# Ten projection chunks of up to 512 columns become eight: regrouping the input projection of a two-layer decoder trunk

## The chip, the cores and the metric

The kernel runs on one core of one Trainium2 chip. The metric is the device time of one execution in microseconds (us); lower is better. A core has five engines with a queue each: TensorE (PE, with its weight loads listed as PEld), VectorE (DVE), ScalarE (ACT), GpSimd (POOL) and SyncE (SP), which here issues most of the DMA transfers. Each engine works through its own queue in order and waits for others at semaphores.

## What is computed

Two layers of a decoder trunk on 256 tokens of 1024 channels, in float32. In each layer one input projection feeds three attentions and all gates:

```python
h = rms_norm(x, norm_g)
proj = h @ w_in                                  # 256 x 1024 times 1024 x 7058
(mq, mk, mv, mz, nq, kc, vc, ksl, vsl, kw, vw, ng, nz,
 fq, fk, fv, ff, fz, gl) = jnp.split(proj, offsets, axis=-1)
...
y_moba = (o_moba * jax.nn.silu(mz)) @ w_up_moba      # o_moba: 6 heads of mq, mk, mv
...
y_nsa = (o_nsa * jax.nn.silu(nz)) @ w_up_nsa         # o_nsa: 4 heads of nq, three gated branches
...
log_f = jax.nn.log_sigmoid((ff + b_f).astype(jnp.float32)).transpose(0, 2, 1)
o_fox = merge_heads(fox_attention(q, k, split_heads(fv, FOX_HEADS), log_f))
y_fox = (o_fox * jax.nn.silu(fz)) @ w_up_fox
g = jax.nn.sigmoid(gl + b_gate).reshape(B, S, N_BRANCH, D_MODEL)
merged = g[:, :, 0] * y_moba + g[:, :, 1] * y_nsa + g[:, :, 2] * y_fox
return x + merged @ w_out
```

The fox attention adds to its scores the running sum of log_f at the query less that at the key, so every query needs the running sums of all keys, per head.

## The kernel before

**Dense products.** The 256 tokens are two halves (t = 0, 1) of 128. Both factors of a product are split into a high part of type float32r and the rest, and `mm3` (lines 286 to 289) adds three matmuls: high by high, high by low, low by high. A chunk of w_in of n columns takes 8 row blocks x 2 halves x 3 = 48 matmuls of n columns (`dense`, line 294). Its accumulators are two PSUM banks (`new_acc`, 291) of a pool of four, so a chunk takes over the banks of an earlier chunk once those are evacuated.

**Weights.** A chunk is loaded in tiles of two row blocks (`chunk` 229, `load` 246; staging pool `wst` of six). ACT rounds a tile to its high part (line 262), DVE subtracts it (line 263); `prefetch` has four such tiles split ahead of use.

**Order on PE.** PE's order is written out by hand; Tile orders the other engines' instructions. `run` (1072) lists the chunks. After each step of 3 matmuls, `tick` advances a planner's clock by 3 x n x 0.00042 us, and every unit of work (a generator) that has come due adds its next piece; the yields (LAG_Q = 10, LAG_F = 9 and so on) are the planner's us between a unit's steps. `finish` advances the clock by 0.25 us at a time, with no dense work, until the units named are done.

The chunks are a (queries and compressed tokens of nsa, 512 columns), mv 384, b (396), mq 384, mz 384, mk 384, fv 384, fq 384, fz (ff and fz, 390), fk 384, with the four parts w0 to w3 of the compression weights in between, then six chunks gl0 to gl5 of 512 for the gates gl, then the up projections and the output projection.

**What follows a chunk.** `evac` (439) scales columns of an accumulator by the row's norm into SBUF on ACT. `qk_post` (525) norms and rotates six heads of queries or keys and, LAG_Q later, transposes them. `v_post` and `z_post` evacuate values and output gates. `cmp_post` (773) runs behind w3; the first heads (`nsa_heads`) start when it is done, then the compressed heads (`cmp_heads`, whose PV product is line 857 and waits for a copy `pc`, line 850), then the moba heads and the fox heads. At most two pairs of heads run at a time, and their PV products (lines 587 to 591) keep their order.

**Forget gates.** `fz_post` (863) computes log_f by a series of small DVE operations (lines 870 to 888), sums it along the tokens by three matmuls (891 to 893), writes the sums to DRAM (899) and reads them back to all 128 partitions as `ck` by two broadcasts on ACT's queue (900, 901). DVE adds the causal mask to two of ck's three blocks of 128 columns (908, 909). `attend` (550) takes ck as a bias for the fox heads (line 562).

**Pages.** Pool `pgs` has 12 pages of 4 KB a partition. om (2), hT (4), z (2), mv, fv, Z (2, until w3 is done) and the gates gl (2 per branch, taken by the evacuations in line 926 of gl0, gl2 and gl4) share it.

Of the kernel before, what the change touches and what calls it, by code (L numbers as in the profile page):

```python
# [29 lines left out]
C_NQ, C_KW = 1536, 2048  # L30
C_FQ, C_FK, C_FV, C_FF = 2444, 2828, 3212, 3596
C_GL = 3986
# [61 lines left out]
def trunk(ctx, tc, x, w_in, b_gate, cmp_w1, w_up_moba, w_up_nsa, w_up_fox, w_out, gains_d, eye_d, x_t, small_d, row_d, out):  # L94
# [134 lines left out]
    def chunk(blocks, n):  # L229

        out_ = []
        for block in blocks:
            kk = max(b for _, b, _ in block)
            m = 1024 // n
            for k in range(0, kk, m):
                w_ = {"n": n, "m": min(m, kk - k), "at": len(tiles), "loads": []}
                for a, b, src in block:
                    a1, b1 = max(a, k), min(b, k + m)
                    if a1 < b1:
                        for r, s_ in src if isinstance(src, tuple) else ((slice(0, 128), src),):  # L240
                            w_["loads"].append((r, a1 - k, b1 - k, s_[:, a1 - a:b1 - a]))
# [108 lines left out]
    def layer(l):  # L350
# [139 lines left out]
        def k_cols(k, hi, lo, t, pairs, key):  # L490

            p3, g = cols_of(k, pairs, key)
            for (r, o, d), (_, _, e) in zip(halves(hi, t), halves(lo, t)):
                A.activation(d[r], p3[r], AF.Copy, scale=g[r])
                V.scalar_tensor_tensor(e[r], p3[r], g[r], d[r].bitcast(F32), op0=ALU.mult, op1=ALU.subtract)
                A.activation(d[o], p3[r], AF.Copy, scale=g[r])  # L496

        def shared_cols(k, b, t, key):
# [26 lines left out]
        def qk_post(key):  # L525
# [5 lines left out]
            for t in range(NT):  # L531
                sumsq(ss, ps, t, 0, 6)
            qs = heads_scaled(ps, head_factors(ss, 6), 0, 6, key)
            yield LAG_Q
            for t in range(NT):
                if key[1] == "k":
                    k_cols(qs[t], *sh["T_" + key], t, 3, key)
                else:
                    q_cols(qs[t], *sh["T_" + key], t, 3, key)
                yield LAG_T  # L540

        def v_post(key):
            ps = sh["ps_" + key]
            sh[key] = pgs.tile([128, NT, 384], F32, name="v", tag="page")
            for t in range(NT):
                evac(ps, t, 0, 384, sh[key][:, t, :])
            yield 0
# [159 lines left out]
        def post_b():  # L707
# [45 lines left out]
        def load_w1(i):  # L753
            src = tuple((slice(kv * 64, kv * 64 + 64),
                         cmp_w1[l, kv, i * 8 * HD:(i + 1) * 8 * HD, :].rearrange("(i d) n -> d i n", d=HD))
# [107 lines left out]
        def fz_post():  # L863
            ps = sh["ps_fz"]
            xf = sm.tile([128, NT, FH], F32, name="xf")
# [4 lines left out]
            for t in range(NT):  # L870
                V.scalar_tensor_tensor(xf[:, t, :], ps[t][:, 0:FH], sh["r"][:, t:t + 1], bfb[:, l, :],
                                       op0=ALU.mult, op1=ALU.add)
# [3 lines left out]
            for t in range(NT):  # L876
                evac(ps, t, FH, 384, sh["z"][t][:, 640:1024])

# [113 lines left out]
        def mm_out(parts, between):  # L992
# [18 lines left out]
            for t in range(NT):  # L1011
                for n in range(2):
# [9 lines left out]
        parts = {}  # L1022
        PROJ = {"a": (C_NQ, 512), "b": (C_KW, 396), "mq": (C_MQ, 384), "mk": (C_MK, 384), "mv": (C_MV, 384),
                "mz": (C_MZ, 384), "fq": (C_FQ, 384), "fk": (C_FK, 384), "fv": (C_FV, 384), "fz": (C_FF, 390)}
        ORDER = ["a0", "a1", "mv0", "mv1", "b0", "w0", "b1", "mq0", "w1", "mq1", "w2", "mz0", "mz1", "w3",
                 "mk0", "mk1", "fv0", "fv1", "fq0", "fq1", "fz0", "fz1", "fk0", "fk1"]

        def queue_loads():
            for o in ORDER:
                name, b = o[:-1], int(o[-1])  # L1030
                if name == "w":
                    parts[o] = load_w1(b)
                else:
                    c0, n = PROJ[name]
                    m = 1 if l == 0 and name == "a" else 4
                    parts[o] = chunk([[(i, i + m, rows_of(w, 4 * b + i, 4 * b + i + m, c0, n))
                                       for i in range(0, 4, m)]], n)
            sh["gls"] = [load_gl(c) for c in range(6)]
            sh["ups"] = [load_up(n) for n in range(2)]
            sh["outs"] = load_out()  # L1040

        def mm(o, starts=None):
            name = o[:-1]
            if name == "w":
                return mm_w1(int(o[-1]), parts[o])
            n, h = PROJ[name][1], int(o[-1])
            if h == 0:
# [18 lines left out]

        def z_post():
            for t in range(NT):
                evac(sh["ps_mz"], t, 0, 384, sh["z"][t][:, 0:384])
            yield 0  # L1070

        def run(starts, following):
# [9 lines left out]
            mm("mv1")  # L1082
            uv = unit(v_post("mv"))
            if l == 0:
# [93 lines left out]
```

## Time and profile before

| | us |
|---|---|
| median of three runs | 518.43 |
| lowest, highest | 517.68, 518.47 |
| the profiled execution, whole | 517.28 |
| its span, from the first to the last instruction | 515.5 |
| PE busy in the span | 501.9 (97%) |
| DVE busy | 401.5 (78%) |
| ACT busy | 334.6 (65%) |

The profile records one execution. Busy is the time in which an engine has an instruction under way; matmuls are pipelined, so their printed lengths overlap, and the distance between starts tells what one of them costs the queue. "Idle before" is the time an engine stood before an instruction, and the arrow behind it names what released it. The chain of waits follows the last instruction back through whatever released each step.

### The profile page before, as it was taken

The numbers are of one execution on the slowest core, as the hardware profiler recorded it, in microseconds if no ns is written. First come the engines' busy times: TensorE is split into PE (matmuls) and PEld (weight loads), VectorE is DVE, ScalarE is ACT, GpSimd is POOL, SyncE is SP. The second block draws the span as 40 slices with busy tenths as digits, with TensorE's granted clock in tenths as the row PEclk, the third lists the DMA queues.
The fourth block names the chain that finished last, engine by engine and source line by source line (L and its number), as shares of the span: only waits on it lengthen the run. The fifth ranks groups of instructions, "written<-read, shape, count | busy, mean of one in ns | idle before, by whom it ended". The sixth has DMA issues, their size and how long they took to land.

```text
span 515.5 us, 8244 instructions
## 1 busy us (share of the span) xinstructions
PE 501.9 (97%) x2822; PEld 446.6 (87%) x2822; DVE 401.5 (78%) x846; ACT 334.6 (65%) x645; POOL 60.5 (12%) x84
## 2 busy tenths in 40 slices
PE   8899999999999999999999999999998999999997
PEld 6788999999788888888889989999987888888886
DVE  4799988789876658998497998768997755698953
ACT  4887676976675576654276976678757666655440
POOL 3510211000110005025100000000011000042300
PEclk9999999999999999999999999999999999999999
DMA  8999886555585443756557898647556643537502
GB/s 279 332 243 256 237 246 194 148 166 162 164 257 144 124 129 116 219 163 190 144 145 207 202 244 268 173 127 202 154 182 189 194 130 116 164 117 226 180 9 81
DMA packets 60226, 93.09 MB, mean 181 GB/s; under 512 B 3980, under 2 KB 34840, under 8 KB 60184
## 3 DMA queue, kind: packets, MB, share of 16 engines
q1 hardware_dynamic: 56592, 89.67, 59.7%
q10 hardware_dynamic: 3592, 2.90, 1.7%
q8 instruction: 22, 0.36, 0.3%
q14 instruction: 20, 0.16, 0.1%
HBM read 91.49 MB, written 1.06 MB: 180 GB/s over the span
## 4 chain that ended last, share of the span: by engine, by line
PE 81%; DVE 8%; ACT 5%; DMA 3%; issue 3%; ACTq 0%; DVEq 0%; SPq 0%
PE acc L287 22%; PE acc L289 21%; PE acc L288 21%; DVE wl L263 4%; PE at L579 2%; DMA st<-in_w_in_dram 2%; ACT wh L262 2%; PE at L565 2%; PE at L566 2%; PE at L336 1%; PE o L587 1%; PE o L589 1%; PE o L591 1%; PE at L473 1%; PE o L768 1%
## 5 line engine op out<-in xcount | busy, mean ns | idle before, releaser
L263 DVE TENSOR_TENSOR wl<-st,wh 128x1024 fp32r<-128x1024 f32 (+4 forms) x180 | 200.3, 1120 | 53.7 <-ACT wh L262 52.0
L262 ACT ACTIVATE wh<-st 128x1024 fp32r<-128x1024 f32 (+4 forms) x180 | 170.2, 953 | 86.9 <-PE acc L289 68.0
L287 PE MATMUL acc<-wh,hT 128*128 128x512 f32 (+4 forms) x560 | 216.8, 387 | 1.4 <-ACT wh L262 1.0
L288 PE MATMUL acc<-wl,hT 128*128 128x512 f32 (+4 forms) x560 | 202.6, 362 | 0.9 <-DVE wl L263 0.9
L289 PE MATMUL acc<-wh,lT 128*128 128x512 f32 (+4 forms) x560 | 203.0, 362 | 0.0
L289 PEld LDWEIGHTS acc<-wh,lT 128*128 128x128 f32 x560 | 105.1, 188 | 10.9
L287 PEld LDWEIGHTS acc<-wh,hT 128*128 128x128 f32 x560 | 105.8, 189 | 9.2 <-ACT wh L262 1.4
L288 PEld LDWEIGHTS acc<-wl,hT 128*128 128x128 f32 x560 | 105.9, 189 | 7.8 <-DVE wl L263 1.5
L574 ACT ACTIVATE p<-p,nm 128x128 f32<-128x128 f32 x80 | 35.6, 446 | 24.4 <-DVE nm L572 24.3
L940 POOL TENSOR_TENSOR z<-z,tmp 128x512 f32<-128x512 f32 x8 | 12.9, 1645 | 109.0 <-ACT tmp L937 109.0
L287 PE MATMUL acc<-wh,qkT 128*128 128x512 f32 x64 | 25.6, 400 | 0.0
L289 PE MATMUL acc<-wh,qkT 128*128 128x512 f32 x64 | 25.0, 391 | 0.0
L288 PE MATMUL acc<-wl,qkT 128*128 128x512 f32 x64 | 25.0, 390 | 0.0
L978 POOL TENSOR_TENSOR mg<-mg,tmp 128x512 f32<-128x512 f32 x8 | 15.8, 1997 | 51.5 <-DVE tmp L977 51.5
L579 PE MATMUL at<-ident,p 128*128 128x128 f32 x120 | 19.8, 274 | 0.3
L926 DVE SCALAR_TENSOR_TENSOR gl<-acc,rt,tmp 128x512 f32<-128x512 f32 x24 | 17.3, 745 | 1.8 <-PE o L591 1.1
L579 PEld LDWEIGHTS at<-ident,p 128*128 128x128 f32 x120 | 15.0, 146 | 2.5 <-ACT qkT L496 0.6
L572 DVE CUSTOM_DVE_ANT_0 p<-at,tabs 128x128 f32<-128x128 f32 (+1 forms) x56 | 17.0, 354 | 0.1
L583 DVE COPY pt<-at 128x384 f32<-128x384 f32 x20 | 11.1, 555 | 7.2 <-PE at L579 7.0
L768 PE MATMUL o<-wh,Z 128*63 128x256 f32 x64 | 15.6, 282 | 0.4 <-DVE Z L744 0.3
L581 ACT ACTIVATE pt<-at 128x384 f32<-128x384 f32 x20 | 9.7, 483 | 9.5 <-PE at L579 9.4
L769 PE MATMUL o<-wl,Z 128*63 128x256 f32 x64 | 15.4, 280 | 0.2 <-DVE wl L263 0.2
(238 smaller groups left out, 690.9 us busy)
## 6 DMA issues: line engine op xcount, KB each, us to landing
st<-in_w_in_dram SPq DMA_DIRECT2D x52, 512.0 KB, 3.6
st<-in_w_in_dram SPq DMA_DIRECT2D x56, 384.0 KB, 4.1
st<-in_cmp_w_dram SPq DMA_DIRECT2D x32, 256.0 KB, 4.7
st<-in_w_out_dram SPq DMA_DIRECT2D x16, 512.0 KB, 3.8
st<-in_w_in_dram SPq DMA_DIRECT2D x8, 396.0 KB, 6.9
st<-in_w_in_dram SPq DMA_DIRECT2D x8, 390.0 KB, 3.2
tmp<-in_b_gate_dram SPq DMA_DIRECT2D x12, 256.0 KB, 4.4
st<-in_w_up_moba_dram SPq DMA_DIRECT2D x4, 512.0 KB, 3.6
```

The source lines that it names most:

```text
L262: return (lambda: A.activation(h, s_, AF.Copy), lambda: V.tensor_tensor(lo, s_, h.bitcast(F32), op=ALU.subtract))
L263: lambda: V.tensor_tensor(lo, s_, h.bitcast(F32), op=ALU.subtract))
L287: T.matmul(ps, sh, wh, start=first, stop=False)
L288: T.matmul(ps, sh, wl, start=False, stop=False)
L289: T.matmul(ps, sl, wh, start=False, stop=last)
L572: V.tensor_tensor_reduce(out=u, in0=sp, in1=add[t], scale=-SCALE, scalar=BIG, op0=ALU.add, op1=ALU.min, accum_out=nm)
L574: exps.append(A.activation(u, u, AF.Exp, bias=nm, scale=-1.0, accum_out=rsum[:, t, hb:hb + 1]))
L579: T.transpose(pts[:, s * 128:(s + 1) * 128], p[:, s * 128:(s + 1) * 128], ident)
L768: T.matmul(U, st, h, start=i == 0, stop=False)
L769: T.matmul(U, st, lo, start=False, stop=i == CL - 1)
L926: V.scalar_tensor_tensor(sh["gl"][t][b][:, n * 512:(n + 1) * 512], ps[t], sh["r"][:, t:t + 1], bg, op0=ALU.mult, op1=ALU.add)
L978: (G if b == 1 else V).tensor_tensor(m, m, tmp, op=ALU.add)
```

## The change

The ten projection chunks ahead of gl become eight. Six of them are filled to 512 columns: mv, b and mq each take a piece of mz; mk and fq a piece of fv; fk a piece of fz. The fifth chunk, ff (402 columns), holds the first 128 columns of fv, ff, 256 columns of fz and the last 12 of mz; it stands where mz stood, and `fz_post` follows it. gl0 moves ahead of fk. A tile's columns can now come from several ranges of w_in, by one DMA each. Evacuations follow the pieces. ck is filled by one broadcast; the mask sums read the block that it fills, in `mask_sums`, which is ordered behind the first half of fk's key columns.

```diff
-C_FQ, C_FK, C_FV, C_FF = 2444, 2828, 3212, 3596
+C_FQ, C_FK, C_FV, C_FF, C_FZ = 2444, 2828, 3212, 3596, 3602
...
-        for i, (r, a, b, src) in enumerate(w_["loads"]):
-            queues[i % len(queues)].dma_start(v[r, a:b], src)
+        for i, (r, a, b, c, src) in enumerate(w_["loads"]):
+            queues[i % len(queues)].dma_start(v[r, a:b, c], src)
...
             for t in range(NT):
                 sumsq(ss, ps, t, 0, 6)
+            for t in range(NT):
+                if key == "mq":
+                    evac(ps, t, 384, 128, sh["z"][t][:, 244:372])
+                elif key == "fk":
+                    evac(ps, t, 384, 128, sh["z"][t][:, 896:1024])
+                else:
+                    c = 128 if key == "mk" else 256
+                    evac(ps, t, 384, 128, sh["fv"][:, t, c:c + 128])
             qs = heads_scaled(ps, head_factors(ss, 6), 0, 6, key)
             yield LAG_Q
             for t in range(NT):
                 if key[1] == "k":
-                    k_cols(qs[t], *sh["T_" + key], t, 3, key)
+                    i = k_cols(qs[t], *sh["T_" + key], t, 3, key)
+                    if key == "fk" and t == 0:
+                        mask_sums(i)
...
-        def v_post(key):
+        def v_post():
...
+                evac(ps, t, 384, 128, sh["z"][t][:, 0:128])
...
                 evac(ps, t, 140, 256, sh["z"][t][:, 384:640])
+                evac(ps, t, 396, 116, sh["z"][t][:, 128:244])
...
         def fz_post():
-            ps = sh["ps_fz"]
+            ps = sh["ps_ff"]
+            sh["fv"] = pgs.tile([128, NT, 384], F32, name="v", tag="page")
...
-                evac(ps, t, FH, 384, sh["z"][t][:, 640:1024])
+                evac(ps, t, 0, 128, sh["fv"][:, t, 0:128])
+                evac(ps, t, 128 + FH, 256, sh["z"][t][:, 640:896])
+                evac(ps, t, 390, 12, sh["z"][t][:, 372:384])
...
-            nc.scalar.dma_start(sh["ck"][:, :, 0:128], csd[:, 0:128][None].to_broadcast([128, FH, 128]))
             nc.scalar.dma_start(sh["ck"][:, :, 128:384], csd[None].to_broadcast([128, FH, S]))
...
+        def mask_sums(last):
+
             mask = tabs[:, K_MASK + 128:K_MASK + 256][:, None, :].to_broadcast([128, FH, 128])
-            for i in (0, 256):
-                V.tensor_tensor(sh["ck"][:, :, i:i + 128], sh["ck"][:, :, i:i + 128], mask, op=ALU.add)
+            for i, j in ((0, 128), (256, 256)):
+                after(V.tensor_tensor(sh["ck"][:, :, i:i + 128], sh["ck"][:, :, j:j + 128], mask, op=ALU.add), [last])
...
-        ORDER = ["a0", "a1", "mv0", "mv1", "b0", "w0", "b1", "mq0", "w1", "mq1", "w2", "mz0", "mz1", "w3",
-                 "mk0", "mk1", "fv0", "fv1", "fq0", "fq1", "fz0", "fz1", "fk0", "fk1"]
+        PROJ = {"a": [(C_NQ, 512)], "mv": [(C_MV, 384), (C_MZ, 128)], "b": [(C_KW, 396), (C_MZ + 128, 116)],
+                "mq": [(C_MQ, 384), (C_MZ + 244, 128)], "ff": [(C_FV, 128), (C_FF, 262), (C_MZ + 372, 12)],
+                "mk": [(C_MK, 384), (C_FV + 128, 128)], "fq": [(C_FQ, 384), (C_FV + 256, 128)],
+                "fk": [(C_FK, 384), (C_FZ + 256, 128)]}
+        ORDER = ["a0", "a1", "mv0", "mv1", "b0", "w0", "b1", "mq0", "w1", "mq1", "w2", "ff0", "ff1", "w3",
+                 "mk0", "mk1", "fq0", "fq1", "gl0", "fk0", "fk1"]
...
+        def columns(ranges, k0, k1):
+            at = 0
+            out_ = []
+            for c0, n in ranges:
+                out_.append((slice(0, 128), slice(at, at + n), rows_of(w, k0, k1, c0, n)))
+                at += n
+            return tuple(out_)
...
             mm("w2")
-            mm("mz0")
-            mm("mz1")
-            unit(z_post())
+            mm("ff0")
+            mm("ff1")
+            uf = unit(fz_post())
             mm("w3")
...
-            mm("fv0")
-            mm("fv1")
-            uv = unit(v_post("fv"))
             mm("fq0")
             mm("fq1")
             uq = unit(qk_post("fq"))
-            mm("fz0")
-            mm("fz1")
-            uf = unit(fz_post())
+            mm_gl(0, sh["gls"][0])
             mm("fk0")
             mm("fk1")
             uk = unit(qk_post("fk"))
             hf = pairs(heads3("fq", "fk", "fv", 0, 640, True) + heads3("fq", "fk", "fv", 1, 640, True),
-                       [uq, uk, uv, uf])
+                       [uq, uk, uf])
             every = hs + h2 + [hc] + hm + hf
-            for c in range(5):
+            for c in range(1, 5):
                 mm_gl(c, sh["gls"][c])
             finish(*every)
```

## Rows read from the trace of the kernel before

**Rows 1.** The page: busy shares, granted clock in 40 slices, the chain by engine.

```profile
PE 501.9 (97%) x2822; PEld 446.6 (87%) x2822; DVE 401.5 (78%) x846; ACT 334.6 (65%) x645; POOL 60.5 (12%) x84
...
PEclk9999999999999999999999999999999999999999
...
PE 81%; DVE 8%; ACT 5%; DMA 3%; issue 3%; ACTq 0%; DVEq 0%; SPq 0%
```

**Rows 2.** Timeline of PE, chunk of 384 columns (start, length, engine, line, form).

```profile
84.58 0.34 PE L287 MATMUL acc<-wh,hT 128*128 128x384 f32 x1
...
86.66 0.33 PE L287 MATMUL acc<-wh,hT 128*128 128x384 f32 x1
```

**Rows 3.** Timeline of PE, chunk gl5 of 512 columns.

```profile
203.66 0.39 PE L289 MATMUL acc<-wh,lT 128*128 128x512 f32 x1
...
206.61 0.39 PE L287 MATMUL acc<-wh,hT 128*128 128x512 f32 x1
```

**Rows 4.** Timeline of PE: layer 0's last PV, and the first matmul of gl5.

```profile
195.46 0.33 PE L591 MATMUL o<-v,pt 128*128 128x64 f32 x2
195.60 0.47 PE L287 MATMUL acc<-wh,hT 128*128 128x512 f32 x1
195.91 0.39 PE L288 MATMUL acc<-wl,hT 128*128 128x512 f32 x1
...
201.85 0.39 PE L287 MATMUL acc<-wh,hT 128*128 128x512 f32 x1
```

**Rows 5.** Timeline of DVE in layer 0: second mask sum of ck, copy pc.

```profile
137.09 0.96 DVE L909 TENSOR_TENSOR ck<-ck,tabs 128x768 f32<-128x768 f32 x1 [1.72 <-DMA ck<-csd]
...
139.10 0.48 DVE L850 COPY pc<-at 128x128 f32<-128x128 f32 x2
```

**Rows 6.** Waits of the whole span: us in total, times, longest us.

```profile
PE o L857 <- DVE pc L850: 2.6, 2, 1.5
...
PE at L473 <- DVE kn L465: 2.2, 2, 1.2
```

**Rows 7.** Instructions of tile y: duration ns min/median/max, first and last start.

```profile
L886 DVE TENSOR_SCALAR y<-y x14: 164/173/175, 114.7 to 374.3; 128x12 f32<-128x12 f32 x14
```

**Rows 8.** Stretches of layer 0: length, PE, PEld, DVE, ACT, POOL busy, clock, DMA.

```profile
41.80:52.50 10.70, 9.46 (x61) 9.12 (x60) 9.99 (x25) 7.68 (x19) 0.35 (x2) 1.00 0.99 268
52.50:66.00 13.50, 13.50 (x90) 13.25 (x91) 12.25 (x23) 9.32 (x16) 3.85 (x5) 1.00 0.83 227
```

**Rows 9.** Groups of DVE by form: busy us, mean ns, idle before.

```profile
L263 DVE TENSOR_TENSOR wl<-st,wh 128x1024 fp32r<-128x1024 f32 x100 | 125.8, 1263 | 32.2 <-ACT wh L262 31.7
L263 DVE TENSOR_TENSOR wl<-st,wh 128x768 fp32r<-128x768 f32 x56 | 53.6, 965 | 12.0 <-ACT wh L262 11.0 <-PE acc L289 0.4
```

**Rows 10.** Timeline of PE, first chunks of layer 0: idle time in brackets.

```profile
19.07 0.44 PE L287 MATMUL acc<-wh,hT 128*128 128x384 f32 x1 [0.96 <-ACT wh L262]
20.21 0.44 PE L288 MATMUL acc<-wl,hT 128*128 128x384 f32 x1 [0.69 <-DVE wl L263]
...
34.36 0.30 PE L768 MATMUL o<-wh,Z 128*63 128x256 f32 x1 [0.27 <-DVE Z L744]
...
39.62 0.45 PE L288 MATMUL acc<-wl,hT 128*128 128x396 f32 x1 [0.24 <-DVE wl L263]
```

**Rows 11.** Groups of ACT by form: evacuations.

```profile
L440 ACT ACTIVATE z<-acc,rt 128x384 f32<-128x384 f32 x8 | 4.5, 569 | 2.7 <-PE acc L289 2.7
L440 ACT ACTIVATE kv<-acc,rt 128x128 f32<-128x128 f32 x4 | 1.5, 364 | 1.1 <-DVE rt L319 1.0
```

**Rows 12.** Instructions of line 251: duration ns min/median/max, first and last start.

```profile
L251 SPq DMA_DIRECT2D st<-in_w_in_dram x130: 328/368/793, 1.2 to 437.8; - x130
```

**Rows 13.** Timeline of DVE: evacuations of gl2, gl3 and gl4 in layer 0.

```profile
173.31 0.74 DVE L926 SCALAR_TENSOR_TENSOR gl<-acc,rt,tmp 128x512 f32<-128x512 f32 x1
...
195.83 1.41 DVE L926 SCALAR_TENSOR_TENSOR gl<-acc,rt,tmp 128x512 f32<-128x512 f32 x2 [0.55 <-PE o L591]
...
206.97 1.40 DVE L926 SCALAR_TENSOR_TENSOR gl<-acc,rt,tmp 128x512 f32<-128x512 f32 x2
```

More of the change, by code (lines that the diff above doesn't have):

```diff
@@ L239, in chunk @@
                     if a1 < b1:
-                        for r, s_ in src if isinstance(src, tuple) else ((slice(0, 128), src),):
-                            w_["loads"].append((r, a1 - k, b1 - k, s_[:, a1 - a:b1 - a]))
+                        for r, c, s_ in src if isinstance(src, tuple) else ((slice(0, 128), slice(0, n), src),):
+                            w_["loads"].append((r, a1 - k, b1 - k, c, s_[:, a1 - a:b1 - a]))
                 tiles.append(w_)
@@ L494, in k_cols @@
                 A.activation(d[r], p3[r], AF.Copy, scale=g[r])
-                V.scalar_tensor_tensor(e[r], p3[r], g[r], d[r].bitcast(F32), op0=ALU.mult, op1=ALU.subtract)
+                i = V.scalar_tensor_tensor(e[r], p3[r], g[r], d[r].bitcast(F32), op0=ALU.mult, op1=ALU.subtract)
                 A.activation(d[o], p3[r], AF.Copy, scale=g[r])
+            return i
         def shared_cols(k, b, t, key):
@@ L540, in qk_post @@
                 yield LAG_T
-        def v_post(key):
-            ps = sh["ps_" + key]
-            sh[key] = pgs.tile([128, NT, 384], F32, name="v", tag="page")
+        def v_post():
+            ps = sh["ps_mv"]
+            sh["mv"] = pgs.tile([128, NT, 384], F32, name="v", tag="page")
             for t in range(NT):
-                evac(ps, t, 0, 384, sh[key][:, t, :])
+                evac(ps, t, 0, 384, sh["mv"][:, t, :])
+                evac(ps, t, 384, 128, sh["z"][t][:, 0:128])
             yield 0
@@ L753, in load_w1 @@
         def load_w1(i):
-            src = tuple((slice(kv * 64, kv * 64 + 64),
+            src = tuple((slice(kv * 64, kv * 64 + 64), slice(0, CH),
                          cmp_w1[l, kv, i * 8 * HD:(i + 1) * 8 * HD, :].rearrange("(i d) n -> d i n", d=HD))
@@ L870, in fz_post @@
             for t in range(NT):
-                V.scalar_tensor_tensor(xf[:, t, :], ps[t][:, 0:FH], sh["r"][:, t:t + 1], bfb[:, l, :],
+                V.scalar_tensor_tensor(xf[:, t, :], ps[t][:, 128:128 + FH], sh["r"][:, t:t + 1], bfb[:, l, :],
                                        op0=ALU.mult, op1=ALU.add)
@@ L1022, in layer, with width @@
         parts = {}
-        PROJ = {"a": (C_NQ, 512), "b": (C_KW, 396), "mq": (C_MQ, 384), "mk": (C_MK, 384), "mv": (C_MV, 384),
-                "mz": (C_MZ, 384), "fq": (C_FQ, 384), "fk": (C_FK, 384), "fv": (C_FV, 384), "fz": (C_FF, 390)}
-        ORDER = ["a0", "a1", "mv0", "mv1", "b0", "w0", "b1", "mq0", "w1", "mq1", "w2", "mz0", "mz1", "w3",
-                 "mk0", "mk1", "fv0", "fv1", "fq0", "fq1", "fz0", "fz1", "fk0", "fk1"]
+        PROJ = {"a": [(C_NQ, 512)], "mv": [(C_MV, 384), (C_MZ, 128)], "b": [(C_KW, 396), (C_MZ + 128, 116)],
[4 more added lines that the diff above has]
+                 "mk0", "mk1", "fq0", "fq1", "gl0", "fk0", "fk1"]
+        sh["gls"] = [None] * 6
+        def width(name):
+            return sum(n for _, n in PROJ[name])
+        def columns(ranges, k0, k1):
[5 more added lines that the diff above has]
+            return tuple(out_)
         def queue_loads():
@@ L1032, in queue_loads @@
                     parts[o] = load_w1(b)
+                elif name == "gl":
+                    sh["gls"][0] = load_gl(0)
                 else:
-                    c0, n = PROJ[name]
                     m = 1 if l == 0 and name == "a" else 4
-                    parts[o] = chunk([[(i, i + m, rows_of(w, 4 * b + i, 4 * b + i + m, c0, n))
-                                       for i in range(0, 4, m)]], n)
-            sh["gls"] = [load_gl(c) for c in range(6)]
+                    parts[o] = chunk([[(i, i + m, columns(PROJ[name], 4 * b + i, 4 * b + i + m))
+                                       for i in range(0, 4, m)]], width(name))
+            for c in range(1, 6):
+                sh["gls"][c] = load_gl(c)
             sh["ups"] = [load_up(n) for n in range(2)]
@@ L1045, in mm @@
                 return mm_w1(int(o[-1]), parts[o])
-            n, h = PROJ[name][1], int(o[-1])
+            n, h = width(name), int(o[-1])
             if h == 0:
@@ L1065, in mm_first @@
                           order=[(i, t) for i in range(4)], oldest=parts["a0"][0])
[L1067 to L1070, printed above, removed]
         def run(starts, following):
@@ L1082, in run @@
             mm("mv1")
-            uv = unit(v_post("mv"))
+            uv = unit(v_post())
             if l == 0:
```

## The prediction

> **What bounds the kernel now.** I read the page's busy shares first, then the chain of waits, then TensorE (PE) instruction by instruction. PE is busy 97% of the span, its granted clock is full in every slice (the 2.4 GHz level), and 81% of the chain that ended last is PE's own work [rows 1]. So this is a kernel bound by PE's queue: an edit is worth what it takes out of PE's instructions plus what it takes out of, or puts into, the short waits between them. I therefore cost matmuls by the distance of their starts (their printed lengths overlap), and then went through PE's waits.
>
> A dense matmul 384 columns wide starts 12 steps after another of its kind in 86.66 - 84.58 = 2.08 us, 173.3 ns each [rows 2]; at 512 columns 13 steps take 206.61 - 203.66 = 2.95 us, 226.9 ns [rows 3]. Between these points a column costs 53.6 / 128 = 0.419 ns, and 173.3 - 384 x 0.419 = 12.5 ns of each matmul does not depend on its width.
>
> **Fewer, wider matmuls.** A chunk is 8 row blocks x 2 token halves x 3 products = 48 matmuls. Before, a layer has, beside chunk a, seven chunks of 384, one of 396 (178.3 ns by the same line) and one of 390 (175.8): 48 x (7 x 173.3 + 178.3 + 175.8) = 75.2 us. After: six of 512 and one of 402 (180.8): 48 x (6 x 226.9 + 180.8) = 74.0 us. The columns are the same 3986; 96 matmuls fewer per layer save 1.2 us, **2.4 us** in two layers. This is on PE's path whatever else happens. The Trainium skill (TensorE: Matmul & The Clock Gate, "Wait — 56ns, not 53.3ns?") gives a warm matmul its columns at 2.4 GHz plus about 2.5 ns; by that the 192 matmuls would save 0.5 us, not 2.4. The trace disagrees by a factor of five, 12.5 ns [rows 2, 3], and decides.
>
> Small matmuls of the attention stand between the dense ones, and the first dense matmul behind such a visit takes 195.91 - 195.60 = 0.31 us instead of 0.23 [rows 4]: 0.08 us a visit. A tick now spans 512 columns, so that more pieces come due at one place, and the last four PV steps stand with no dense work between (below): about 3 visits fewer per layer, **0.5 us**.
>
> **Forget gates early, one broadcast, masks behind fk.** Before, VectorE (DVE), which works in order, stands 1.72 us before the second mask sum of ck until the broadcast has landed, spends 0.96 us on the sum, and only later reaches the copy pc [rows 5]. PE stands idle before the PV of the compressed heads (L857) until pc is there: 2.6 us in the two layers [rows 6]. After, fz_post runs behind ff, some 390 + 512 + 512 + 512 columns earlier than the first use of ck, and the mask sums are ordered behind the first key columns of fk. Nothing waits for the broadcast there: a second DMA on ScalarE's (ACT's) queue goes, and the two sums (1.9 us of DVE) lie behind L857 rather than ahead of it. Bounds: all 2.6 us go, or none if a weight split then stands ahead of pc. I take **2.2 us**, since 1.72 + 0.96 us of DVE ahead of pc exceed the wait.
>
> The price is paid earlier: fz_post's chain is some 23 small DVE operations of 0.17 us [rows 7], 4 to 5 us with their hand-overs, now between mq's post-processing and cmp_post. DVE is busy 9.99 of 10.7 us and 12.25 of 13.5 us in these stretches [rows 8]. PE's matmuls of cmp_post and of the running sum are placed by fixed lags and would wait. Below: no wait, since the extra columns of mv, b and mq (372, about 8 us of PE) let DVE arrive with less backlog. Above: 1.2 us a layer, what PE lost at kn in a stretch as full [rows 6]. I take 0.4 a layer, **0.8 us lost**.
>
> **The first chunks.** The 372 more columns ahead of mq's end put 8 us of dense work, at the same share of split work per column (1263 ns per 1024 columns against 965 per 768 [rows 9]), between the same post-processing steps of a and b. PE's wait for kn (2.2 us in two layers [rows 6]) should mostly close: 1.6 us. The waits for Z and for wl in chunk b (0.27 and 0.24 us in layer 0 [rows 10]) close: 0.5 us. Against it, the first tile of mv is 1024 wide instead of 768, comes by two DMAs, and PE stands before its wh and its wl [rows 10]: the DVE split alone is 0.30 us longer, ACT's and the loads' share as much again: 0.6 us. Net **1.5 us won**; bounds 2.7 won and, if the b posts wait for the two more evacuations, 1.5 lost.
>
> **Evacuations and queues.** z and fv now come in pieces: per layer 8 evacuations of 384 columns (0.57 us) become 2 of these, 2 of 256 and 16 of 128 or fewer (0.36 us) [rows 11]: 3.4 us more ACT per layer. ACT is idle 35% of the span [rows 1], and the users of z and fv come tens of us later; cost nothing. What hides it is the lag of 10 planner us between qk_post and its transposes; without that, 0.73 us per chunk. Loads: some 24 more DMAs per layer on SyncE's queue at 0.37 us of issue [rows 12]; SyncE issues well ahead, because loads are released six staging tiles back. Nothing.
>
> **Where the heads end.** This is what the change makes late. w3, behind which the first attention heads start, now stands behind 2450 instead of 2060 columns, since ff comes after four full chunks; the heads themselves follow each other by their own lags. So the heads end 390 columns later against an unchanged sum of columns up to the end of gl4: 390 x 48 x 0.443 ns (226.9 / 512) = 8.3 us. Before, the last PV of layer 0 starts at 195.46, and gl5's first matmul at 201.85 [rows 4]: 6.4 us of slack. After, the heads end about 1.9 us of dense work past gl4, in `finish`, where no dense matmul is left to run.
>
> Idle PE there is short, since the transposes of the last head stand two tiles before gl4's end. But a second thing hangs on it. The pool of 12 pages is full in gl2 (om 2, hT 4, z 2, mv, fv, gl 2), and gl2's second token half waits for fv's page, that is for the last PV: its evacuation L926 runs at 195.83, after PE's L591, and not near the first half's at 173.31 [rows 13]. Until then two of four accumulators are held. Before, they came free 5 us ahead of gl5; after, gl5's first matmul waits for the last PV's end (0.33 us), that evacuation (0.7 us) and the hand-overs: 1.1 us, and 0.2 for a split that DVE may be in: 1.3 us a layer, **2.6 us lost**. Bounds: 0.7 a layer (evacuation alone) and 3.8 (below).
>
> **Sum.** -2.4 - 0.5 - 2.2 + 0.8 - 1.5 + 2.6 = -3.2 us. The profiled execution took 517.28 us (span 515.5, 1.8 around it); it would take 514.1. The median shown is 518.43, 1.15 above that execution, so I expect a median of 515.2.
>
> **The rivals.**
> 1. *Page chain at the up projection (slower).* gl4's own evacuations need the pages of z, which come free behind sigmoid, GpSimd's product and DVE's product: they start 206.97 - 195.46 = 11.5 us after the last PV [rows 4, 13], 12.9 us to their end. After, gl5 begins about 1.3 us and ends 13.1 us behind gl4, and the up projection needs those accumulators then. The chain just fits. If DVE's queue, which has the closing of the last heads and the evacuations of gl2 and gl3 in it at once, makes it longer by two splits (2.5 us), PE stands for it in both layers: 515.2 + 5.0 = 520.2. It decides from 13 us of chain. For it: the margin is 0.2 us; against it: splits run four tiles ahead and can yield.
> 2. *DVE stays full from b to mk:* waits move instead of closing. The first chunks give nothing (+1.5) and the forget gates cost their upper bound (+1.6): 518.3, no change.
> 3. *Masks were not what L857 waited for:* another split takes their place; +2.2, 517.4.
> 4. *The width-independent part is 2.5 ns:* 192 x 10 ns less gain, 517.1. The page named above says this; the starts of [rows 2, 3] speak against it.
> 5. *More is hidden than I think:* L857's wait closes wholly (-0.4), the first chunks give their upper bound (-1.2), fz_post costs nothing (-0.8) and the end of the heads its lower bound (-1.2): 511.6.
>
> **How the numbers follow.** Forecast 0.50 (own range 513 to 517), rival 1 0.12, 2 0.14, 3 0.06, 4 0.06, 5 0.12. A measurement of this kernel can tell about 0.2% from no change, 1.04 us: below 517.4 is faster, above 519.5 slower. The forecast puts 0.48 below and 0.02 within; rival 5 all below; rivals 3 and 4 half to two thirds below, 0.07, and 0.05 within; rival 2 0.02 below, 0.09 within, 0.03 above; rival 1 all above. Faster 0.69, same 0.16, slower 0.15. Leaving out the top of rival 1 and the bottom of rival 5, the range is 511.3 to 519.8.
>
> **What would show it.** All dense projections but ff step at 227 ns, and PE runs 192 matmuls fewer. No idle before L857; DVE's L909 without a wait for ck. PE's wait at kn below 0.5 us. The last L591 of each layer behind the last matmul of gl4, and gl5's first matmul waiting 1 to 2 us for DVE L926. I am wrong if PE waits at L792 or at the running sum by over 1 us, if the first matmul of the up projection waits for an evacuation of gl4, or if the heads end inside gl4.

## The result and the profile after

The changed kernel takes 531.29 us (median; 529.88 to 533.55) beside 518.05 us of the kernel before (518.43 above is the median of three executions, this one of four): ratio 1.0259, 95% interval 1.0232 to 1.0285. It is 13.2 us slower, where 515.2 was forecast. The profiled execution took 530.92 us, its span 529.0.

The page of the changed kernel (busy us, share, instructions; granted clock in 40 slices; DMA packets; the chain by engine), answering to [rows 1]:

```profile
PE 505.5 (96%) x2630; PEld 424.2 (80%) x2630; DVE 402.2 (76%) x830; ACT 335.7 (63%) x653; POOL 65.8 (12%) x84
...
PEclk9998979999999999999999999899999999999999
...
DMA packets 71713, 92.30 MB, mean 174 GB/s; under 512 B 8812, under 2 KB 46328, under 8 KB 71672
...
PE 75%; DVE 11%; DMA 8%; ACT 4%; issue 2%; ACTq 0%; SPq 0%; DVEq 0%
```

PE runs 192 matmuls fewer, as forecast, and yet is busy longer: the clock row, full in every slice before, now dips early in layer 0 and again in layer 1. DMA has grown from 3% of the chain to 8%. PE's waits (us in total, times, longest; line numbers of the changed kernel) answer to [rows 6]:

```profile
PE acc L288 <- DVE wl L263: 4.6, 3, 2.5
PE acc L287 <- ACT wh L262: 4.0, 2, 2.9
PE acc L289 <- DVE qkT L342: 3.2, 2, 1.6
PE at L792 <- ACT zf L788: 2.2, 2, 1.7
PE at L591 <- DVE nm L584: 2.1, 2, 1.1
PE acc L287 <- DVE gl L944: 1.7, 2, 0.8
```

(L342 is the low part of `transpose_split`, L788 cmp_post's copy of U, L584 a head's score maximum, L944 the evacuation of gl, L926 before. The matmul that the prediction calls L792 is L805 here; L792 is now the one ahead of it.) The two waits that [rows 6] showed, for pc and for kn, are gone. Waits for weight tiles stand first, all in layer 0; of them 1.1 us for wh and 0.8 for wl stand at mv, where 1.0 and 0.7 stood before. The others come in both layers: at the layer's end for qkT (the transposes of the gated heads) and for gl, and ahead of that for zf behind ff and for nm in the first heads. Timeline of PE around the waits for weights (start, length, idle before in brackets):

```profile
40.52 0.48 PE L287 MATMUL acc<-wh,hT 128*128 128x512 f32 x1
43.52 0.65 PE L288 MATMUL acc<-wl,hT 128*128 128x512 f32 x1 [2.52 <-DVE wl L263]
...
65.32 0.28 PE L782 MATMUL o<-wl,Z 128*63 128x256 f32 x1
68.50 0.70 PE L287 MATMUL acc<-wh,hT 128*128 128x402 f32 x1 [2.90 <-ACT wh L262]
70.42 0.70 PE L288 MATMUL acc<-wl,hT 128*128 128x402 f32 x1 [1.23 <-DVE wl L263]
...
72.26 0.54 PE L287 MATMUL acc<-wh,hT 128*128 128x402 f32 x1
72.60 0.54 PE L288 MATMUL acc<-wl,hT 128*128 128x402 f32 x1
72.93 0.54 PE L289 MATMUL acc<-wh,lT 128*128 128x402 f32 x1
```

PE stands at the first tile of b1 and again at the first of ff. Behind it the steps are 0.33 us, not the 0.181 worked out for 402 columns (0.184 once the clock is full again): TensorE runs at its 1.2 GHz level. The stretches (length; PE, PEld, DVE, ACT, POOL busy; granted clock; DMA share; GB/s) show the clock that was granted behind each stand, the last one in layer 1 behind the wait at L792:

```profile
40.50:46.00 5.50, 2.98 (x11) 2.06 (x10) 5.37 (x7) 4.83 (x9) 0.00 (x0) 0.79 0.91 195
65.30:72.00 6.70, 2.57 (x9) 1.89 (x8) 5.79 (x15) 3.70 (x6) 2.29 (x3) 0.67 0.64 147
72.00:81.00 9.00, 9.00 (x45) 8.92 (x44) 4.53 (x5) 3.18 (x3) 0.00 (x0) 0.86 0.99 305
338.00:345.00 7.00, 5.31 (x20) 4.25 (x20) 6.77 (x17) 4.08 (x8) 0.00 (x0) 0.76 0.98 299
```

At 65.30 to 72.00 DVE is busy but the DMA engines have room (0.64), so it is not bandwidth that is missing there. SyncE's queue over ff's loads (start, length from the first to the last of the group, count), and behind it a row of its waits:

```profile
50.45 8.51 SPq L251 DMA_DIRECT2D st<-in_w_in_dram  x4
59.96 0.61 SPq L251 DMA_DIRECT2D st<-in_cmp_w_dram  x1
60.62 6.31 SPq L251 DMA_DIRECT2D st<-in_w_in_dram  x7
```

```profile
SPq L251 <- DMA st<-in_w_in_dram: 14.4, 22, 2.7
```

Four issues take 8.5 us: they are the first ranges (fv's 128 columns) of all four ff tiles, one by one as buffers come free. Only then follow the second and third ranges. PE needs the first whole tile at 65.4. Its third range, 12 columns, was issued at 64.00, 0.01 us behind the landing of its second, and landed at 67.47. ACT's row for ff's tiles starts there, and PE follows at 68.50:

```profile
67.57 2.40 ACT L262 ACTIVATE wh<-st 128x804 fp32r<-128x804 f32 x3 [1.31 <-DMA st<-in_w_in_dram]
```

At b1 the last step was another: wh was there, but DVE came to wl's subtraction only at 42.24, behind some 4 us of other work.

```profile
42.24 3.49 DVE L263 TENSOR_TENSOR wl<-st,wh 128x1024 fp32r<-128x1024 f32 x3
```

And SyncE waits 14.4 us for weight loads to land; in the kernel before the same wait is 2.8 us in 4 cases. By the trace's records 20 of the 22 cases are of two kinds. In 9 (7.8 us), all at ff, a range waits for the landing of the range ahead of it in the same tile. In 11 (5.2 us) a load waits for the landing of the one that SyncE issued eight before it and whose semaphore it uses: the load issued at 26.54 stood until 26.48, when the one issued at 19.52 had landed. With two or three loads to a tile, eight loads are fewer tiles.

The tail, behind two rows of a chunk at full clock (timeline of PE):

```profile
84.31 0.39 PE L289 MATMUL acc<-wh,lT 128*128 128x512 f32 x1
...
85.67 0.39 PE L289 MATMUL acc<-wh,lT 128*128 128x512 f32 x1
...
209.76 0.39 PE L603 MATMUL o<-v,pt 128*128 128x64 f32 x2
210.99 0.50 PE L287 MATMUL acc<-wh,hT 128*128 128x512 f32 x1 [0.84 <-DVE gl L944]
...
223.22 0.39 PE L288 MATMUL acc<-wl,qkT 128*128 128x512 f32 x1
225.20 0.50 PE L289 MATMUL acc<-wh,qkT 128*128 128x512 f32 x1 [1.59 <-DVE qkT L342]
```

Six steps take 85.67 - 84.31 = 1.36 us, 227 ns each, as in [rows 3]. The heads end past gl4 and gl5 waits for the evacuation, as forecast (compare [rows 4]); the up projection then waits for the low half of the gated heads' transposes. DVE comes to them behind three splits:

```profile
221.07 3.48 DVE L263 TENSOR_TENSOR wl<-st,wh 128x1024 fp32r<-128x1024 f32 x3
224.47 1.28 DVE L342 TENSOR_TENSOR qkT<-at,qkT 128x512 fp32r<-128x512 f32 x2
```

### The profile page after: what moved, and what is told of

The parts are those of the page before. It is cut to its first block, busy times and chain, and to the rows that moved or that the text cites. A ratio compares the mean times of both kernels' runs of the same rounds, so it can differ in the third digit from the quotient of the medians.

```text
span 529.0 us, 7888 instructions
## 1 busy us (share of the span) xinstructions
PE 505.5 (96%) x2630; PEld 424.2 (80%) x2630; DVE 402.2 (76%) x830; ACT 335.7 (63%) x653; POOL 65.8 (12%) x84
## 3 DMA queue, kind: packets, MB, share of 16 engines
HBM read 90.71 MB, written 1.06 MB: 173 GB/s over the span
## 4 chain that ended last, share of the span: by engine, by line
PE 75%; DVE 11%; DMA 8%; ACT 4%; issue 2%; ACTq 0%; SPq 0%; DVEq 0%
PE acc L287 20%; PE acc L289 19%; PE acc L288 19%; DMA st<-in_w_in_dram 6%; DVE wl L263 5%; PE at L591 3%; DVE om L959 2%; ACT wh L262 2%; PE at L577 2%; PE at L578 1%; PE o L599 1%; PE o L603 1%; PE o L601 1%; PE at L473 1%; DMA st<-in_cmp_w_dram 1%
## 5 line engine op out<-in xcount | busy, mean ns | idle before, releaser
L263 DVE TENSOR_TENSOR wl<-st,wh 128x1024 fp32r<-128x1024 f32 (+2 forms) x164 | 198.8, 1219 | 67.5 <-ACT wh L262 63.1
L262 ACT ACTIVATE wh<-st 128x1024 fp32r<-128x1024 f32 (+2 forms) x164 | 167.6, 1027 | 92.2 <-PE acc L289 59.4
L287 PE MATMUL acc<-wh,hT 128*128 128x512 f32 (+1 forms) x496 | 207.4, 418 | 5.9 <-ACT wh L262 4.0
L288 PE MATMUL acc<-wl,hT 128*128 128x512 f32 (+1 forms) x496 | 194.0, 391 | 4.6 <-DVE wl L263 4.6
L289 PE MATMUL acc<-wh,lT 128*128 128x512 f32 (+1 forms) x496 | 194.0, 391 | 0.0
L287 PEld LDWEIGHTS acc<-wh,hT 128*128 128x128 f32 x496 | 95.0, 191 | 20.4 <-ACT wh L262 4.7
L288 PEld LDWEIGHTS acc<-wl,hT 128*128 128x128 f32 x496 | 95.0, 192 | 17.1 <-DVE wl L263 5.6
L944 DVE SCALAR_TENSOR_TENSOR gl<-acc,rt,tmp 128x512 f32<-128x512 f32 x24 | 17.1, 740 | 9.0 <-PE o L603 7.7
L444 ACT ACTIVATE sq<-acc,rt 128x384 f32<-128x384 f32 (+2 forms) x28 | 13.7, 488 | 12.0 <-PE acc L289 8.6
L584 DVE CUSTOM_DVE_ANT_0 p<-at,tabs 128x128 f32<-128x128 f32 (+1 forms) x56 | 17.1, 349 | 1.4 <-PE at L578 1.3
L289 PEld LDWEIGHTS acc<-wh,qkT 128*128 128x128 f32 x64 | 12.0, 188 | 7.0 <-DVE qkT L342 4.5
L445 DVE TENSOR_REDUCE ss<-sq 128x6 f32<-128x384 f32 (+2 forms) x28 | 12.1, 433 | 6.1 <-ACT sq L444 5.7
```

What stands on the lines that cost most here:

```text
L262: return (lambda: A.activation(h, s_, AF.Copy), lambda: V.tensor_tensor(lo, s_, h.bitcast(F32), op=ALU.subtract))
L263: lambda: V.tensor_tensor(lo, s_, h.bitcast(F32), op=ALU.subtract))
L287: T.matmul(ps, sh, wh, start=first, stop=False)
L288: T.matmul(ps, sh, wl, start=False, stop=False)
L289: T.matmul(ps, sl, wh, start=False, stop=last)
L444: A.activation(sq, ps[t][:, col:col + nh * HD], AF.Square, scale=sh["r"][:, t:t + 1])
```

## Experiments

Ratios are to the kernel before on the same chip, with 95% intervals. Three causes were on the table: the loads in ranges (1), DVE and ACT crowded between b and mk (2), and heads that end late (3).

**One range per tile.** w_in's columns are laid out beforehand in the order of the chunks.

```diff
+    cols = np.concatenate([np.arange(c, c + n) for name in PROJ for c, n in PROJ[name]] + [np.arange(C_GL, 7058)])
+    a["w_in"] = np.ascontiguousarray(a["w_in"][:, :, cols])
```

> The changed kernel with the columns of w_in laid out beforehand in the order in which the chunks use them, so that a tile is again one DMA; chunks, order on PE and all evacuations stay. Theory 1 (loads in pieces: SyncE issues the pieces of ff's four tiles out of tile order behind waits, PE stands 2.8 us at its first tile of b1 and 3.1 + 1.7 + 0.3 us at ff, and its clock falls to half behind both): these 7.9 us and 2 to 5 us of slow clock go, 531.3 becomes 519 to 522, and the granted clock is 1.00. Theory 2 (crowded ACT and DVE and late heads are the whole loss, the loads only show it): 528 to 531, the waits at ff stay for wh or wl. Under both the waits at L944 (1.06 a layer) and for qkT (1.75 a layer) stay.

520.39 us, ratio 1.0066 (1.0038 to 1.0094), mean granted clock 0.997. Of the 2.59% some 1.9% go with the ranges: 10 us, by the intervals 8 to 12. Behind the first tile of mv no wait for wl or wh is left; what the page of waits still lists first is the tail and the heads, unchanged:

```profile
PE acc L301 <- DVE qkT L354: 3.2, 2, 1.6
PE at L603 <- DVE nm L596: 2.1, 2, 1.1
PE acc L299 <- DVE gl L956: 1.7, 2, 0.8
```

**Ranges in order.** Each load on SyncE's queue is ordered behind the one ahead of it in the code.

```diff
+            if q is nc.sync:
+                after(d, last_load[-1:])
+                last_load.append(d)
```

> The changed kernel with all pieces, but every weight load on SyncE's queue is ordered behind the one ahead of it in the code, so a tile's pieces are issued together. If it is the order of the pieces on the queue that starves ff: ff's 5.1 us and the slow clock behind it go, the 2.8 us at b1 may stay: 522 to 525. If it is the number or the small size of the packets (half of the rows are 48 to 512 bytes long): ff still waits, 528 to 531.

548.95 us, 1.0633 (1.057 to 1.0696): far slower, which neither case expected. SyncE's queue, and its waits:

```profile
57.51 12.19 SPq L253 DMA_DIRECT2D st<-in_w_in_dram  x8
```

```profile
SPq L253 <- DMA st<-in_w_in_dram: 45.8, 31, 4.4
```

Eight loads take 12.2 us because five of them stand until the range ahead of them in the same tile has landed. In the program the second range of an ff tile waits for the landing of the first and the third for the second, although they write different columns; ranges of the 512 wide tiles carry no such wait. So I read the odd order in the changed kernel as the scheduler's way around that chain; no run shows why it chose it.

**The ranges without the chain.** All ranges stay; ff's tiles, and their high and low parts, lie in SBUF at 512 columns a row block instead of 402, and then the program has no wait between the ranges of a tile.

```diff
+    def rows(a, n):
+        return a[:, 0:1024].rearrange("p (k n) -> p k n", n=512)[:, :, 0:n] if n == 402 else \
+            a[:, 0:1024 // n * n].rearrange("p (k n) -> p k n", n=n)
...
```

> The changed kernel with all its pieces, sizes and packets, but ff's tiles lie in the staging buffer at 512 columns a row block instead of 402. In the run with ordered loads each piece of an ff tile was issued only when the piece ahead of it had landed (57.99 landed 60.57, next 60.59 landed 63.23, next 63.24); pieces of the 512 wide tiles were not (77.44 and 78.03). With 512 columns a block the program no longer has that wait. If this chain of three landings per ff tile is what starves ff: as the run with relaid columns, 519 to 523, ff's 3.1 + 1.7 us gone, the 2.8 us at b1 may stay. If the count and size of the packets starve it: 527 to 531.

523.11 us, 1.0130 (1.0098 to 1.0161). SyncE's queue, and its waits:

```profile
47.88 9.81 SPq L255 DMA_DIRECT2D st<-in_w_in_dram  x12
```

```profile
SPq L255 <- DMA st<-in_w_in_dram: 5.6, 11, 1.0
```

All twelve loads of ff are out by 57.7, and PE no longer stands at ff. None of SyncE's 11 waits is for a range of the same tile; nine are for the load issued eight before. So the chain costs 1.3% (6.7 us, by the intervals 4.5 to 8.8), half of the whole result. The other effects of the ranges cost 0.64% (3.3 us, by the intervals 1 to 5.5), by comparison with one range per tile: in this profile b1 still waits 1.7 us for wl, w3 2.2 us. That the eight loads are what makes them late fits the queue's waits; no run varied their number.

**Ranges in the kernel before.** Six chunks come in two ranges, fz in three.

```diff
+        CUTS = {"mv": (0, 256, 384), "b": (0, 280, 396), "mq": (0, 256, 384), "mk": (0, 256, 384),
+                "fq": (0, 256, 384), "fk": (0, 256, 384), "fz": (0, 128, 378, 390)}
```

> The kernel before, its chunks, order and evacuations untouched, but six of its chunks loaded in two ranges of columns and fz in three (128, 250 and 12 columns) per tile, as in the changed kernel: 64 DMAs more. If pieces alone cost time whatever the chunks are: PE waits at fz and fk, where the issue order interleaves, for several us: 521 to 528. If they hurt only where DVE and ACT are crowded as well (the stretch b to mk of the changed kernel): 518 to 519.5.

516.57 us, 0.9998 (0.9972 to 1.0024): no change. From the page, and from SyncE's waits:

```profile
DMA packets 77635, 93.11 MB, mean 181 GB/s; under 512 B 9100, under 2 KB 52248, under 8 KB 77592
```

```profile
SPq L251 <- DMA st<-in_w_in_dram: 10.1, 17, 1.7
```

There are more small packets than in the changed kernel (60226 packets in the kernel before), and SyncE waits 10.1 us for landings. Of these, 7.2 us are the same chain, in fz's tiles of 390 columns; the tiles of 384 and 396 columns in two ranges carry no such wait. PE does not stand at fz. I read that as loads running far enough ahead there, while ff follows w2, whose tiles PE uses up in 0.9 us each. But the unchanged time is also a balance: PE's waits for weights grow by 2.2 us (b1's wl from 0.2 to 1.0, a part of the compression weights by 1.2), and its waits for kn (2.2 us) and, in layer 0, for pc (1.0 us) are gone. So the run shows that neither packets nor ranges must lengthen the kernel, not that they are free.

**Heads early.** On top of one range per tile, w1 to w3 half a chunk earlier each, w3 ahead of ff, gl0 behind fk.

```diff
...
-"b1", "mq0", "w1", "mq1", "w2", "ff0", "ff1", "w3", "mk0", "mk1", "fq0", "fq1", "gl0", "fk0", "fk1"
+"b1", "w1", "mq0", "w2", "mq1", "w3", "ff0", "ff1", "mk0", "mk1", "fq0", "fq1", "fk0", "fk1", "gl0"
...
```

> As the run with relaid columns, with w1, w2 and w3 half a chunk earlier each, w3 ahead of ff (so the first heads start behind 2048 columns, 2060 before the change, 2450 in it), and gl0 behind fk, as before the change. The last PV of a layer then stands as far ahead of gl4's end as before the change. If late heads cost the tail: the waits for L944 (1.06 a layer) and for qkT at the up projection (1.75 a layer) go, 5.6 us below the run with relaid columns; with fz_post behind cmp_post rather than ahead of it, the wait at L792 (0.7 and 1.9 us) goes as well: 513 to 515. If the tail waits come from the pages or the chain behind the heads whatever their place: within 1.5 us of that run.

519.89 us, 1.0058 (1.0021 to 1.0095), no better than one range per tile. The number is that of the second case, but its reason is not: both tail waits are gone, in both layers. In their place:

```profile
PE at L485 <- DVE kn L477: 2.2, 2, 1.6
PE at L603 <- DVE qkT L499: 2.0, 2, 1.0
...
PE at L817 <- DVE hs L812: 1.4, 1, 1.4
...
PE at L919 <- DVE y L916: 1.1, 1, 1.1
```

Cause 3 is confirmed: its 5.6 us go when the heads end earlier, and they were paid back in the stretch of cause 2. By the order written for PE, two edits make the heads late, w3 behind ff and gl0 ahead of fk, which holds the fox heads; no run moved one of them alone.

**ff and fz_post late.** As the last one, ff where fz stood.

```diff
...
-"w3", "ff0", "ff1", "mk0", "mk1", "fq0", "fq1", "fk0", "fk1", "gl0"
+"w3", "mk0", "mk1", "fq0", "fq1", "ff0", "ff1", "fk0", "fk1", "gl0"
...
```

> As the run with early heads, with ff and fz_post moved back to where fz stood, ahead of fk. If fz_post's 23 small DVE operations and the 12 extra evacuations between mq and mk are what makes PE wait there (kn 0.76 and 1.78, hs 1.6, the running sum 0.7 and 1.25 us in that run): these go, 4 to 6 us below that run, 0.994 to 0.998 of the kernel before. If the closer weight parts w1 to w3 crowd DVE, kn and hs stay: within 1.5 us of that run.

523.50 us (executions from 519.64, the profiled one, to 524.04), 1.0113 (1.0065 to 1.0161): no gain, so the first case is out. hs and the running sum stopped waiting, but kn stayed (2.2 us), and PE waited 4.5 us for DVE's q and k columns (`PE at L605 <- DVE qkT L499`); mk and fq now follow mq without a light chunk between. So fz_post is one load among several there. That the closer weight parts are another is what the second case expected; the wait for kn fits it.

**w3 between the halves of ff,** w1 and w2 where the change has them, gl0 behind fk; and **w3 directly behind w2**.

```diff
...
-"w2", "ff0", "ff1", "w3", "mk0"
+"w2", "ff0", "w3", "ff1", "mk0"
...
```

> As the run with relaid columns, with w3 between the halves of ff and gl0 behind fk; w1 and w2 stay where the change has them. The last PV of a layer comes 0.4 chunks (about 4.5 us) earlier than in the run with relaid columns, in the run with early heads it came 0.8 chunks earlier. If the tail's waits (1.06 and 1.75 us a layer) are the price of late heads alone, and what the run with early heads paid instead (kn 0.76 and 1.78, hs 1.6, the running sum 1.25) came from w1 and w2 standing closer: 5 to 6 us below the run with relaid columns, 0.994 to 0.998 of the kernel before. If whatever pulls the heads forward is paid back in DVE's full stretch: 1.004 to 1.008 of the kernel before.

> As the run before this one, but w3 directly behind w2, ahead of ff: heads at the places of the run with early heads, w1 and w2 at the places of the change. Four tiles of compression weights are then used in 16 x 2 x 0.115 = 3.7 us of PE and need four splits of 1.26 us on DVE: up to 1.4 us a layer of waiting for wl, if the four tiles that are split ahead don't cover it. If early heads are free of charge otherwise: as the run with w3 between the halves or up to 2 us above it. If DVE's full stretch takes its price: 1.004 to 1.008 of the kernel before.

522.43 us, 1.0113 (1.0084 to 1.0142), and 528.77 us, 1.0230 (1.0191 to 1.0269), both above every case expected. PE's wait for kn (L485) is gone in both and gl5's wait too; the up projection's wait for qkT is gone in the second run and stays in the first (3.0 us). But now PE stands 2.7 us a layer at the running sum, 3.6 us in the second run. DVE of the first run ahead of that wait, and PE behind it:

```profile
86.33 0.17 DVE L913 TENSOR_TENSOR y<-y,d 128x12 f32<-128x12 f32 x1
86.53 0.34 DVE L827 TENSOR_SCALAR kc<-at,rsc 15x128 f32<-15x128 f32 x1
...
87.46 1.21 DVE L275 TENSOR_TENSOR wl<-st,wh 128x1024 fp32r<-128x1024 f32 x1
88.59 0.18 DVE L913 TENSOR_TENSOR y<-y,d 128x12 f32<-128x12 f32 x1
...
90.05 0.17 DVE L916 TENSOR_TENSOR y<-mn,y 128x12 f32<-128x12 f32 x1
```

```profile
90.32 0.58 PE L919 MATMUL at<-tabs,y 128*6 128x128 f32 x2 [2.69 <-issue]
```

(The trace puts this wait down to "issue", meaning nothing that it shows, but the same one in layer 1 to y, and PE starts 0.1 us behind y's end.) fz_post's chain shares DVE with cmp_post's chain and with splits of 1.2 us, and a matmul of PE was placed by a fixed lag.

**The lag.** As the first of these two, LAG_F 16 instead of 9.

> As the run with w3 between the halves of ff, with one constant changed: the matmuls of the running sum are placed 16 planner us behind the start of fz_post instead of 9. That run waited 2.9 us a layer there for y, the end of fz_post's chain on DVE. If the chain is merely late and nobody needs the sums before the fox heads: 5 to 6 us less, 0.999 to 1.002 of the kernel before. If DVE's backlog at that place holds the next hand-over instead (cmp_post's steps, the first heads' nm): less than 2.5 us gained, 1.006 to 1.011.

518.18 us, 1.0004 (0.9983 to 1.0025): 1.1% less than the run with w3 between the halves, 5.6 us, for one constant. Nobody needed the sums at 9. What is left:

```profile
PE acc L301 <- DVE qkT L354: 3.0, 2, 1.5
PE at L844 <- POOL kc L835: 2.0, 2, 1.0
```

**The forget gates alone,** in the kernel before: one broadcast, masks behind fk's first key columns.

```diff
-            for i in (0, 256):
-                V.tensor_tensor(sh["ck"][:, :, i:i + 128], sh["ck"][:, :, i:i + 128], mask, op=ALU.add)
+        def mask_sums(last):
...
+            for i, j in ((0, 128), (256, 256)):
+                after(V.tensor_tensor(sh["ck"][:, :, i:i + 128], sh["ck"][:, :, j:j + 128], mask, op=ALU.add), [last])
```

> The kernel before with the forget gates' edits alone: ck filled by one broadcast, the two mask sums behind fk's first key columns; fz_post stays where it was. If the mask sums and their wait for the second broadcast held back pc: the waits at L857 (1.2 and 1.7 us) go, 2.2 to 2.9 us less than the kernel before. If another DVE step stands there in their place: no change to 0.5 us.

513.47 us beside 516.2 on that chip, 0.9941 (0.9918 to 0.9965): about 3 us less. The wait at L857 is gone, and kn's (2.1 us) stays. This version beats both kernels.

**Half of the regrouping on top of it:** fv's columns fill mk, fq and fk; the chunk fv goes; one range per tile.

```diff
-                 "mk0", "mk1", "fv0", "fv1", "fq0", "fq1", "fz0", "fz1", "fk0", "fk1"]
+                 "mk0", "mk1", "fq0", "fq1", "fz0", "fz1", "fk0", "fk1"]
```

> The kernel before with the forget gates' edits (0.994 of it by themselves) and only the later half of the regrouping: fv's columns fill mk, fq and fk to 512, the chunk fv goes, w_in is laid out so that each tile is one DMA; mv, b, mq, mz, the compression weights, fz and gl0 stay where they were, so the heads end where they did. 48 matmuls fewer per layer at 12.5 ns are 1.2 us. If wider chunks pay where they make nothing late: 0.991 to 0.993 of the kernel before. If the evacuations in pieces and the larger splits behind mk cost as much as they save: 0.994 to 0.997.

517.9 us, 1.0000 (0.9986 to 1.0013): 0.6% (3 us) worse than the forget gates alone, and above both cases, though 96 matmuls fewer run. New among PE's waits:

```profile
PE at L599 <- DVE qkT L498: 1.9, 2, 0.9
...
PE acc L298 <- DVE qn L520: 1.7, 2, 0.8
```

L520 reads fq's accumulators, which fk takes over. 1.9 + 1.7 us, and 0.7 at cmp_post, are the 3.0 lost and the 1.2 that the matmuls should have brought. That the chunk fv had given DVE time between two query or key chunks is my reading of it; no run put a light chunk back without its columns.

## Why the prediction was wrong

The terms of the sum came out like this (us, two layers; from start to start of PE's instructions in the two profiles; the loads and the second value for the forget gates from the runs):

| step | forecast | measured |
|---|---|---|
| fewer, wider matmuls | -2.4 | -1.6 |
| fewer visits | -0.5 | -0.2 |
| forget gates, masks behind fk | -2.2 | -2.9; alone, 3.0 less |
| first chunks: kn | -1.6 | -2.5 |
| first chunks: waits in b; first tile of mv | +0.1 | -0.8 |
| fz_post early | +0.8 | +2.9 (L792 2.5, running sum 0.4) |
| first heads: nm | none | +2.5 |
| evacuations and queues | 0 | +10 (clock included) |
| end of the heads | +2.6 | +5.6 |

They add to 13.0 of the 13.2 us measured, but that closeness is partly luck: the 10 us are known to 2, and 1.2 us of L792's wait stand in two rows, since with one range per tile it is 1.0 instead of 2.2 us. What was to be seen was seen where the mechanism held: steps of 227 ns, 192 matmuls fewer, no wait for pc or kn, gl5 behind the evacuation. Of the signs that I gave for being wrong, two came nearly as written: PE waits over 1 us in cmp_post (1.7 in layer 1), at the matmul ahead of the one named, and the up projection's first block waits, for another tile. The largest cause was on no list.

**The step that failed** is "SyncE issues well ahead, because loads are released six staging tiles back. Nothing." The 24 DMAs' issue time was indeed nothing. What I did not cost is that a load can wait for the landing of another: the ranges of one tile for each other, 6.7 us by the run that took that chain away, and 3.3 us for the other effects of the ranges, where the queue's waits are for the load issued eight before. [rows 12] gave the price of an issue, not of a landing; the first loads of [rows 10], which PE waited for at the start, were the hint that landings can bind. No rival had it either.

**The clock** was held full, as in [rows 1]. It fell behind PE's stands at b1, at ff and, in layer 1, at L792; at 72 to 81 us, 9.00 us of busy PE at 0.86 are 1.3 us by themselves. My estimate from the granted clock where it was low (0.54 at 43.5 to 47.2, 0.51 at 68.5 to 74.6, 0.61 at 339.8 to 344.2) is 5 to 6 us in all. Those waits cost more than their length.

**fz_post** was right in place and too small in size: I took 0.4 a layer, with 1.2 as the upper bound. With one range per tile, PE waits 0.5 us a layer at that matmul of cmp_post and 0.2 at the running sum; the changed kernel's further 1.2 us there go with the ranges. The wait for zf is one for ACT, which comes to the copy behind ff's evacuations and two splits: the evacuations in pieces, which I put at nothing, are part of it. The first heads' wait for nm I did not foresee. It comes at 115.64, 20 us behind fz_post's last step (94.67), and is gone or under 0.3 us a layer in the runs whose heads start earlier; which work makes it is not shown. In the order with w3 between ff's halves the chain cost more, not by its own 4 to 5 us, but by what stands between its links: 1.2 us splits and another chain. There the lag run shows that most of the price is not DVE's work but PE's fixed place for a matmul that nobody needed yet. In the changed kernel that place costs 0.4 us.

**The end of the heads** was right in mechanism. gl5 waited for L944 by 1.06 us from start to start, 1.1 to 1.3 forecast. Rival 1's place came in as well, 1.75 a layer, but not by its chain: gl4's evacuations end at 221.15, 11.4 us behind the last PV and not 12.9, and the up projection does not wait for them. It waits for the transposes' low halves, which stand behind three 1.2 us splits on DVE. Both waits stay inside the bound of 3.8 a layer that I gave, which was worked out from splits on DVE. gl0 ahead of fk, a second reason for late heads by the written order, was not in the working.

**Forget gates** held. **Matmuls** held in kind, 1.6 us and not 2.4: the undisturbed steps are 228.8 ns on average at 512 columns (the two rows gave 226.9) and 184.1 at 402, beside 173.9 at 384, 179.8 at 396 and 176.7 at 390; by these averages 9 ns of a matmul do not depend on its width, not 12.5. The visits did not: the first dense steps behind small matmuls are longer by 15.1 us in all before and by 14.9 after.

The largest part of the loss is thus ff's three ranges. Without it the regrouping still gives nothing in the orders tried: the version with one range per tile, earlier heads and a longer lag is at 1.0004, though it holds the forget gates' edits, worth 3 us alone.

## What to carry to other kernels

When a tile comes by several DMAs, look at what each of them waits for: the queue runs in order, so one false wait on a landing holds every load behind it. Ask too how many loads are let run at once. In a kernel bound by one engine's queue, a light piece of work between two heavy ones may be cover for the other engines (argued here, not shown); before it is merged away, list what has to be done in its time. A separate edit with its own gain (here the forget gates, 0.6%) should be timed alone.

## What the runs showed of the hardware

TensorE went on at half its clock behind its stands of 2.5 us at b1 (43.5 to 47.2, granted clock 0.54), of 2.9 and 1.2 us at ff (68.5 to 74.6, 0.51; steps of 0.33 us at 402 columns) and of 1.7 us at L792 in layer 1 (339.8 to 344.2, 0.61); behind the 1.6 us at the up projection it did not (225.20 to 225.77 at full steps). Adding 64 DMAs and 17409 packets to the kernel before left its time where it was (0.9998), with more waiting for weights and less for other tiles in the profile. SyncE's loads used eight semaphores in turn, and a load stood until the one issued eight before it had landed (19 such waits, 12.5 us, in the changed kernel). In tiles of 402 and of 390 columns a row block, in three ranges, the program made a range wait for the landing of the one ahead of it; in tiles of 512 columns, and in two ranges of 384 and 396, it did not.
